# A hybrid decoder layer on one core: a head's loads issued a piece at a time, a branch's values in four groups, and the combination's first step pinned in program order

## The chip, the cores and the metric

The kernel runs on one core of a Trainium2 chip. The core has five engines that each work through a queue of instructions in order and wait for each other through semaphores: TensorE (PE, matrix products), VectorE (DVE), ScalarE (ACT), GpSimd (POOL) and SyncE (SP), whose queue issues nearly all DMA transfers. The metric is the device time of one execution in microseconds (us).

## The reference

One layer of a decoder with two kinds of token mixer, batch 1, 2048 tokens, width 1024, float32:

```python
nx = rmsnorm(h, attn_norm_g[l])
proj = jnp.einsum('bsd,dp->bsp', nx, w_in[l])
...
o_a = gla_mixer(...)                 # 4 heads, chunks of 64, low-rank forget gate
...
o_b = dilated_mixer(dq, dk_, dv_, rel_bias)   # 8 heads of 64
mixed = jnp.concatenate([o_a, o_b], axis=-1)
h = h + jnp.einsum('bsm,md->bsd', mixed, w_out[l])
nm = rmsnorm(h, mlp_norm_g[l])
a = jnp.square(jax.nn.relu(jnp.einsum('bsd,df->bsf', nm, w_ff1[l])))
h = h + jnp.einsum('bsf,fd->bsd', a, w_ff2[l])
return rmsnorm(h, final_norm_g)
```

The change lies in the dilated mixer. Each of its 8 heads has three branches (window, dilation) = (128, 1), (512, 4), (2048, 16): a query sees the keys at distances 0, d, 2d, ... up to the window. Each branch gives an output and the log-sum-exp of its logits, and the three are combined with weights from a softmax over those:

```python
for window, dilation in DSA_PATTERN:
    o, lse = dilated_branch(q, k, v, rel_bias, window, dilation)
    outs.append(o); lses.append(lse)
w = jax.nn.softmax(jnp.stack(lses, axis=0), axis=0)
return jnp.sum(w[..., None] * jnp.stack(outs, axis=0), axis=0)
```

## The kernel before, in words

The kernel has stages, one behind the other: the input projection, the attention (both mixers, interleaved; in the profiled execution from about 588 to 957 us), the output projection with the second norm, and the two products of the MLP. Matrix products that need float32 accuracy are split into a high and a low part and done as three matmuls (lines 67 to 69). The change touches the attention stage.

**Units.** A head's branch has 16 query windows of 128. The windows are grouped in `Unit`s: 4 windows for the branch of dilation 16 (called br 2), 2 for the others (br 1, br 0). A head has 20 units, the stage 160. The order is head by head, br 2, 1, 0; the last pair of heads has the order (6, br 2), (6, br 1), (7, br 2), (7, br 1) and then br 0 of both heads in turn.

**The loop** (L952 to L973) runs over k, a software pipeline of three steps: the scores of unit k + AHEAD (3), the transposition of the weights of unit k, and the products with the values of unit k − LAG (2). `Unit.scores` does two score matmuls for a window (L631 and L633: each of the split parts k1, k2 of the keys), and VectorE adds the bias and takes the minimum for the softmax (L643), ScalarE the exponential (L644). `Unit.transpose` transposes the weights on TensorE (L653) and copies them from PSUM by ScalarE (L660) or VectorE (L662). `Unit.values` multiplies with the values (L672), and VectorE copies four windows' result into `O` (L675). Between these stand the steps of the gated linear attention (GLA, lines 754 to 854).

**Calls by unit.** `at_unit(n, f)` (L903) has `f` called in the iteration that does the scores of unit n. `issue_later(n, ...)` (L737) has a transfer issued n iterations later. `first` is the first unit of a branch. So placed are:
- `load_head` (L524): six transfers of 512 KB on SyncE (the queries `qs` twice, two parts of the keys twice each), all at first − 13; the first branch of the next head needs them.
- `pack_q` (L574): four copies by GpSimd that order a head's queries for br 2 and br 1, at first − 4 to first − 1.
- `load_v` (L536): the values of a pair of heads for one branch, one transfer for br 2 and br 0, sixteen of 64 KB for br 1 (L547). Called for the next pair when a branch of the odd head ends (`after`, L892).
- `store_branch` (L681): the outputs of br 2 and br 1 of a pair go to DRAM (`boD`) 3 iterations after the branch's end, because the branches have different orders of tokens.
- `combine_load` (L691): two transfers of 528 KB read the two branches' outputs of half the tokens back, in order of tokens (`cmb`, L696).
- `combine` (L699): the weights. VectorE takes minima (L707, L708), subtracts (L710), ScalarE takes the exponential, VectorE sums and divides (L712 to L718); the small results lie in one tile, `small`. Then GpSimd multiplies (L724) and adds (L726), 128x512 elements at a time, and the result is stored for the output projection. The last group of the last pair runs on VectorE in place of GpSimd.

For pairs 0 to 2 the combination of a pair runs beside the next pair's first head, in two halves: loads at first − 2 and first + 5, six steps each from first + 3 and first + 10. For the last pair it runs beside br 0, in four groups of steps.

**What sets the order.** The instructions aren't run in the order in which the program records them: a scheduler reorders each engine's queue within the data dependences, by a model of its own. An instruction can thus stand ahead of those that were recorded before it. `tc.keep_in_program_order(x)` pins an instruction behind the one recorded before it on its engine. Large buffers come from a pool of 25 slots of equal size (`slot`), which all kinds of data share; a load into a slot waits until its last user has read it.

Of the kernel before, what the change touches and what calls it, by code (L numbers as in the profile page):

```python
# [10 lines left out]
F32 = mybir.dt.float32  # L11
FR = mybir.dt.float32r
I32 = mybir.dt.int32
AF = mybir.ActivationFunctionType
OP = mybir.AluOpType
AX = mybir.AxisListType

S = 2048
D = 1024
NT = S // 128  # L20
# [10 lines left out]
AHEAD, LAG = 3, 2  # L31
# [10 lines left out]
def emit(tc, a, stop=99):  # L42
    nc = tc.nc
    V, A, G, T, SP = nc.vector, nc.scalar, nc.gpsimd, nc.tensor, nc.sync
# [6 lines left out]
    def ps(tag):  # L51
        return psum.tile([128, 512], F32, name="ps_" + tag, tag=tag, bufs=BANKS[tag])

    def slot(name, dt=F32, n=SLOT):

        return up.tile([128, SLOT], dt, name=name, tag="u", bufs=25)[:, :n]

    def view(t, shape):
        n = int(np.prod(shape))
        names = "abcd"[:len(shape)]  # L60
        return t[:, :n].rearrange(f"p ({' '.join(names)}) -> p {' '.join(names)}", **dict(zip(names, shape)))
# [73 lines left out]
    qD = [dram.tile([2, 128, S], F32, name=f"qD{p}") for p in range(4)]  # L135
    kD = [dram.tile([2, 128, S], F32, name=f"kD{p}") for p in range(4)]
# [385 lines left out]


    def load_head(h):  # L524
        pr, hh = divmod(h, 2)
        qs, k1, k2 = slot("qs", FR, S), slot("k1", FR, S), slot("k2", FR, S)
        rows = slice(64 * hh, 64 * hh + 64)
        halves = [slice(64 * dup, 64 * dup + 64) for dup in range(2)]
        for dup, half in enumerate(halves):
            SP.dma_start(qs[half].bitcast(F32), qD[pr][dup, rows])  # L530
        for part, t in enumerate((k1, k2)):
            for half in halves:
                SP.dma_start(t[half].bitcast(F32), kD[pr][part, rows])
        return qs, k1, k2

    def load_v(pr, br):  # L536

        vt = view(slot("v"), (NT, 130))
        G.memset(vt[:, :, 0:130:129], 1.0)
        v = vt[:, :, 1:129]  # L540
        src = vD[:, pr * 128:pr * 128 + 128]
        if br == 0:
            SP.dma_start(v, src.rearrange("(t p) n -> p t n", p=128))
        elif br == 1:
            w = src.rearrange("(b x r i) n -> b x i r n", b=4, r=4, i=8)
            for n in range(NT):
                SP.dma_start(v[:, n], w[n // 4, :, :, n % 4])  # L547
        else:
            SP.dma_start(v, vN[:, pr * 128:pr * 128 + 128].rearrange("(p r) n -> p r n", r=16))
        return vt  # L550
# [130 lines left out]
    def store_branch(pr, br, O):  # L681
        dst = boD[pr][br - 1]
        if br == 1:
            issue_later(3, dst.rearrange("(b p r) n -> p b (r n)", b=4, r=4),
                        O.rearrange("p (b r) n -> p b (r n)", b=4))
        else:
            issue_later(3, dst.rearrange("(p r) n -> p (r n)", r=16), O.rearrange("p r n -> p (r n)"))
# [3 lines left out]
    def combine_load(pr, half):  # L691

        ts, u = slice(8 * half, 8 * half + 8), slot("cmb")
        R = [view(u[:, 1056 * b:], (8, 132)) for b in range(2)]
        for b in range(2):
            SP.dma_start(R[b], boD[pr][b].rearrange("(t p) n -> p t n", p=128)[:, ts])  # L696
        return R

    def combine(pr, t0, n, loaded, X):  # L699

        ts = slice(t0, t0 + n)
        R = [outs[pr, 0][:, ts], *[r[:, t0 % 8:t0 % 8 + n] for r in loaded]]
        at = small[:, t0 // 4 % 2 * 48:] if n == 4 else small
        E, Z, M = view(at, (3, n, 2)), view(at[:, 6 * n:], (2, n, 2)), view(at[:, 10 * n:], (n, 2))
        nm = [r[:, :, 130:132] for r in R]
        den = [r[:, :, 0:130:129] for r in R]
        V.tensor_tensor(M, nm[0], nm[1], op=OP.min)  # L707
        V.tensor_tensor(M, M, nm[2], op=OP.min)  # L708
        for b in range(3):
            V.tensor_tensor(E[:, b], M, nm[b], op=OP.subtract)  # L710
        A.activation(E, E, AF.Exp)
        V.tensor_tensor(Z[:, 0], E[:, 0], den[0], op=OP.mult)  # L712
        for b in (1, 2):
            V.tensor_tensor(Z[:, 1], E[:, b], den[b], op=OP.mult)
            V.tensor_tensor(Z[:, 0], Z[:, 0], Z[:, 1], op=OP.add)
        V.reciprocal(Z[:, 1], Z[:, 0])
        for b in range(3):
            V.tensor_tensor(E[:, b], E[:, b], Z[:, 1], op=OP.mult)  # L718
        yield
        for t in range(0, n, 4):  # L720
            rs = [r[:, t:t + 4, 1:129].rearrange("p t (h e) -> p t h e", h=2) for r in R]
            for b, r in enumerate(rs):
                wb = E[:, b, t:t + 4].unsqueeze(3).to_broadcast([128, 4, 2, 64])
                X.tensor_tensor(r, r, wb, op=OP.mult)  # L724
                if b:
                    X.tensor_tensor(rs[0], rs[0], r, op=OP.add)  # L726
                    yield
        if pr < 3 or t0 >= 8:
            issue_later(3 if pr < 3 else 2,
                        mixD[:, 512 + 128 * pr:640 + 128 * pr].rearrange("(t p) n -> p t n", p=128)[:, ts],  # L730
                        R[0][:, :, 1:129])

    due, clock = [], [0]

    def issue_later(n, *args):

        due.append((clock[0] + n, args))  # L737
# [128 lines left out]
            V.tensor_tensor(w[:, 1], raw, w[:, 0].bitcast(F32), op=OP.subtract)  # L866
            WO.append(w)

    pairs, outs = {0: load_head(0)}, {}
    for part in range(4):  # L870
        pack_q(0, 2, part)
    ring["pes"], ring["pts"] = view(slot("pe"), (4, 512)), view(slot("pt"), (4, 512))
    vs = {}
# [19 lines left out]
    def after(b):  # L893
        pr, hh = divmod(b.h, 2)
        if hh and b.br:
            store_branch(pr, b.br, b.O)
        if hh and pr < 3:
            vs[pr + 1, b.br] = load_v(pr + 1, b.br)

    units = []  # L900
    plan = {}
# [1 line left out]
    def at_unit(n, *f):  # L903
        plan.setdefault(n, []).append(f)
# [3 lines left out]
    def combine_at(pr, t0, n, at, steps):  # L908

        if at is not None:  # L910
            at_unit(at + AHEAD, lambda: got.update({(pr, t0 // 8): combine_load(pr, t0 // 8)}))

        def step():
            if (pr, t0) not in running:
                running[pr, t0] = combine(pr, t0, n, got[pr, t0 // 8], V if (pr, t0) == (3, 12) else G)
            next(running[pr, t0], None)

        for k in steps:
            at_unit(k + AHEAD, step)

    for pr in range(4):
        seq = [(hh, br) for hh in range(2) for br in (2, 1, 0)]
        if pr == 3:
            seq = [(0, 2), (0, 1), (1, 2), (1, 1), (0, 0), (1, 0)]
        for hh, br in seq:
            b = Branch()
            b.h, b.br = 2 * pr + hh, br
            m = 4 if br == 2 else 2
            first = len(units)
            if br:  # L930
                for part in range(4) if first else ():
                    at_unit(first - 4 + part, pack_q, b.h, br, part)
            if br == 2 and first:
                at_unit(first - 13, lambda h: pairs.update({h: load_head(h)}), b.h)
                if hh == 0:
                    for half in range(2):
                        combine_at(pr - 1, 8 * half, 8, first - 2 + 7 * half, [first + 3 + 7 * half + n for n in range(6)])
            if (pr, br) != (3, 0):
                for n in range(0, NT, m):
                    units.append(Unit(b, range(n, n + m)))  # L940
            elif hh:
                for n in range(0, NT, 4):
                    for w in (was, b):
                        units.extend(Unit(w, range(n + k, n + k + 2)) for k in (0, 2))
                for n, at in ((0, 8), (4, 11), (8, 14), (12, 18)):
                    combine_at(3, n, 4, first + 5 + n // 8 if n % 8 == 0 else None, [first + at + k for k in range(4)])
            was = b
    NU = len(units)
    for i in range(8):
# [179 lines left out]
    for at, t in enumerate(tiles):  # L1129
# [3 lines left out]
        h = u[:, 1]  # L1133
        p = [ps("a"), ps("a")]
# [159 lines left out]
    for at in range(7, len(jobs1)):  # L1294
# [12 lines left out]
        if at in (len(jobs1) - 4, len(jobs1) - 2):  # L1307
            n = (at + 4 - len(jobs1)) // 2
# [5 lines left out]
    for ph, (j, half) in enumerate(phases):  # L1314
        P = [bank() for _ in range(4)]
        for k in range(8):
            n = 8 * ph + k
            prep_a(n + 2)
            at = k + 8 * (1 - half)
# [51 lines left out]
def build(nc, inputs, stop=99):  # L1371
    arrays, aps = {}, {}
    for name in _INS:
        arrays[name] = np.ascontiguousarray(inputs[name])
    arrays.update(_constants())
    for name, v in arrays.items():
        aps[name] = nc.dram_tensor(name, v.shape, mybir.dt.from_np(v.dtype), kind="ExternalInput").ap()
    aps["out"] = nc.dram_tensor("out", (1, S, D), F32, kind="ExternalOutput").ap()
    with tile.TileContext(nc, schedule_with_timeline_sim=True) as tc:
        emit(tc, aps, stop)  # L1380
    return arrays
# [10 lines left out]
```

## Time and profile before

| | us |
|---|---|
| median of 3 runs | 2397.13 (2396.92 to 2399.54) |
| the profiled execution | 2398.99 |
| its span in the trace | 2397.2 |
| attention stage | 588.46 to 957.10 |

The span runs from the first to the last instruction that the profile shows; some 1.8 us of the execution lie outside. A line of the profile names the source line, the engine, the operation and the tiles (`out<-in`), then partitions x elements and type. In a timeline, the bracket at the end tells how long the engine was idle before the instruction, and what released it. In a list of waits the three numbers are us in total, times, and the longest. "SPq" is SyncE's queue, whose time on a DMA line is that of issuing, not of transfer.

### The profile page before, as it was taken

Reading aid. Unit: us, or ns where it says so; the run is one execution under the profiler, and the core shown is the slowest. Engines: PE = TensorE matmul, PEld = TensorE weight load, DVE = VectorE, ACT = ScalarE, POOL = GpSimd, SP = SyncE. Lnnn points to the kernel's source line nnn. Section 1 sums busy time; section 2 is a strip of 40 time slices with the busy share of each in tenths; the row PEclk is TensorE's granted clock in tenths of the full one; section 3 lists DMA queues with packets and bytes.
Section 4 is the critical chain, followed back from the end, with each engine's and each line's share of the span. In section 5 each row is a group of like instructions: output and inputs, shape, how many; then the busy total and the mean of one; then the engine's idle time right before and its main releaser. Section 6 shows DMA issues by size and latency. Waiting matters only on the chain.

```text
span 2397.2 us, 35124 instructions
## 1 busy us (share of the span) xinstructions
PE 2306.6 (96%) x12648; PEld 1989.9 (83%) x12648; DVE 1561.9 (65%) x2879; ACT 1148.0 (48%) x2181; POOL 583.3 (24%) x551
## 2 busy tenths in 40 slices
PE   6999998999999989999999999999999999999998
PEld 5877898779989988888788887888888888888886
DVE  6878666765667668445677778877773455556555
ACT  5565434533767657223455556555563333224323
POOL 5555435446566665100000000000000100001002
PEclk9999999999999999999999999999999999999999
DMA  6457664757888867468664447544467496457653
GB/s 159 120 164 230 213 189 136 206 166 194 213 193 226 225 174 241 154 201 267 203 206 145 145 149 242 176 162 157 155 203 274 155 315 208 168 170 248 217 167 106
DMA packets 342540, 458.13 MB, mean 191 GB/s; under 512 B 19620, under 2 KB 215733, under 8 KB 336094
## 3 DMA queue, kind: packets, MB, share of 16 engines
q1 hardware_dynamic: 313614, 413.15, 56.0%
q10 hardware_dynamic: 28752, 42.74, 5.2%
q8 instruction: 99, 1.62, 0.3%
q14 instruction: 75, 0.61, 0.1%
HBM read 293.51 MB, written 167.02 MB: 192 GB/s over the span
## 4 chain that ended last, share of the span: by engine, by line
PE 77%; DMA 8%; DVE 7%; issue 3%; ACT 3%; POOL 1%; SPq 1%; ACTq 0%; POOLq 0%; DVEq 0%
PE ps_a L67 8%; PE ps_a L68 8%; PE ps_a L69 8%; PE ps_c L67 7%; PE ps_c L69 7%; PE ps_c L68 7%; PE ps_d L67 4%; PE ps_d L69 4%; PE ps_d L68 4%; PE ps_a L672 4%; PE ps_o L67 3%; PE ps_o L68 3%; PE ps_o L69 3%; PE ps_d L653 2%; DMA cmb<-boD 2%
## 5 line engine op out<-in xcount | busy, mean ns | idle before, releaser
L1226 POOL TENSOR_TENSOR suma<-suma,gs 128x512 f32<-128x512 f32 x16 | 23.3, 1472 | 1152.6 <-ACT scr L1224 1152.5
L346 DVE TENSOR_TENSOR ca<-ra,ca 128x1024 fp32r<-128x1024 f32 x112 | 137.7, 1230 | 164.4 <-ACT ca L345 164.4
L345 ACT ACTIVATE ca<-ra 128x1024 fp32r<-128x1024 f32 x112 | 118.0, 1054 | 225.8 <-PE ps_c L69 185.4
L345 ACT ACTIVATE w1comb<-w1raw 128x512 fp32r<-128x512 f32 x224 | 139.6, 627 | 158.7 <-PE ps_c L69 57.7
L644 ACT ACTIVATE pe<-pe,O 128x256 f32<-128x256 f32 (+1 forms) x384 | 157.6, 454 | 89.1 <-DVE O L643 76.3
L672 PE MATMUL ps_a<-v,pt 128*128 128x65 f32 x1200 | 185.1, 258 | 13.3 <-DVE pt L662 8.5
L672 PEld LDWEIGHTS ps_a<-v,pt 128*128 128x128 f32 x1200 | 180.9, 200 | 16.1 <-DVE pt L662 9.5
L346 DVE TENSOR_TENSOR w1comb<-w1raw,w1comb 128x512 fp32r<-128x512 f32 x224 | 153.6, 689 | 53.4 <-ACT w1comb L345 53.2
L653 PE MATMUL ps_d<-ident,pe 128*128 128x128 f32 x600 | 160.9, 284 | 0.0
L643 DVE CUSTOM_DVE_ANT_0 pe<-ps_c,nb 128x256 f32<-128x256 f32 (+1 forms) x384 | 126.6, 360 | 43.4 <-PE ps_d L653 20.6
L204 DVE TENSOR_TENSOR wcomb<-wraw,wcomb 128x512 fp32r<-128x512 f32 (+2 forms) x84 | 101.2, 1210 | 70.3 <-ACT wcomb L202 68.8
L202 ACT ACTIVATE wcomb<-wraw 128x512 fp32r<-128x512 f32 (+2 forms) x126 | 96.3, 773 | 103.7 <-PE ps_a L69 20.8
L345 ACT ACTIVATE cb<-rb 128x1024 fp32r<-128x1024 f32 x56 | 59.4, 1061 | 158.0 <-PE ps_o L68 108.1
L67 PE MATMUL ps_c<-hb,w1comb 128*128 128x512 f32 x336 | 132.2, 393 | 2.8 <-ACT hb L345 2.8
L68 PE MATMUL ps_c<-hb,w1comb 128*128 128x512 f32 x336 | 132.2, 393 | 1.6 <-DVE w1comb L346 1.6
L69 PE MATMUL ps_c<-hb,w1comb 128*128 128x512 f32 x336 | 131.8, 392 | 0.0
L67 PE MATMUL ps_c<-cb,ca 128*128 128x512 f32 x336 | 130.8, 389 | 0.0
L68 PE MATMUL ps_c<-cb,ca 128*128 128x512 f32 x336 | 130.8, 389 | 0.0
L69 PE MATMUL ps_c<-cb,ca 128*128 128x512 f32 x336 | 130.8, 389 | 0.0
L653 PEld LDWEIGHTS ps_d<-ident,pe 128*128 128x128 f32 x600 | 111.1, 190 | 0.4
L94 POOL TENSOR_TENSOR stats<-stats,mhalf 128x1 f32<-128x1 f32 (+1 forms) x64 | 46.4, 730 | 259.3 <-DVE stats L93 216.1
L346 DVE TENSOR_TENSOR cb<-rb,cb 128x1024 fp32r<-128x1024 f32 x56 | 68.2, 1221 | 62.5 <-ACT cb L345 62.3
(351 smaller groups left out, 7330.2 us busy)
## 6 DMA issues: line engine op xcount, KB each, us to landing
ra<-actD SPq DMA_DIRECT2D x56, 1024.0 KB, 6.8
actD<-acc SPq DMA_DIRECT2D x192, 256.0 KB, 2.3
rb<-w_ff SPq DMA_DIRECT2D x72, 512.0 KB, 4.8
w1raw<-w_ff SPq DMA_DIRECT2D x32, 1024.0 KB, 7.3
k<-kD SPq DMA_DIRECT2D x32, 512.0 KB, 11.5
rb<-hTD SPq DMA_DIRECT2D x14, 1024.0 KB, 5.9
wraw<-w_in SPq DMA_DIRECT2D x48, 256.0 KB, 3.4
boD<-O SPq DMA_DIRECT2D x8, 1056.0 KB, 6.2
```

Source lines behind the costliest of these rows:

```text
L67: T.matmul(out, sh, mh, start=first, stop=False)
L68: T.matmul(out, sl, mh, start=False, stop=False)
L69: T.matmul(out, sh, ml, start=False, stop=last)
L94: G.tensor_tensor(r2, r, mhalf[:, :n], op=OP.pow)
L202: A.activation(hi, src, AF.Copy, scale=sc)
L204: V.tensor_tensor(lo, src, hi.bitcast(F32), op=OP.subtract)
L345: A.activation(hi, src, AF.Copy)
L346: V.tensor_tensor(lo, src, hi.bitcast(F32), op=OP.subtract)
L643: V.tensor_tensor_reduce(p, s, bias, scale=1.0, scalar=BIG, op0=OP.add, op1=OP.min, accum_out=nm)
L644: A.activation(p, p, AF.Exp, bias=nm, scale=-1.0)
L653: T.transpose(pb[:, i * 128:i * 128 + 128], src, ident)
L672: T.matmul(self.b.opsum[:, n % 4], self.pt[:, i * 128:i * 128 + 128], self.b.v[:, blk, cols], start=first, stop=last)
```

## The change

Six edits, all in the attention stage:

1. `load_head` becomes a generator that issues one of its six transfers a step. They are issued at first − 14, −13, −11, −9, −7 and −5, where all six stood at first − 13. Head 0's come all at once, as before.
2. The sixteen transfers of `load_v` for br 1 are issued in four groups of four, one unit apart, for pairs 1 to 3. For pair 0 they stay together.
3. The store of br 1's outputs is issued 2 iterations after the branch's end, not 3.
4. The first instruction of `combine` (L707) is pinned in program order.
5. For pairs 0 to 2, the combination's loads are issued at first − 3 and first + 3 (before: first − 2 and first + 5), and the second half's steps begin at first + 9 (before: first + 10). The first half's steps stay.
6. For the last pair, the loads are issued at first + 4 and first + 5 (before: first + 5 and first + 6), and the four groups' steps begin at 10, 13, 16, 18 units behind first (before: 8, 11, 14, 18).

```diff
     def load_head(h):
+
         pr, hh = divmod(h, 2)
-        qs, k1, k2 = slot("qs", FR, S), slot("k1", FR, S), slot("k2", FR, S)
         rows = slice(64 * hh, 64 * hh + 64)
-        halves = [slice(64 * dup, 64 * dup + 64) for dup in range(2)]
-        for dup, half in enumerate(halves):
-            SP.dma_start(qs[half].bitcast(F32), qD[pr][dup, rows])
-        for part, t in enumerate((k1, k2)):
-            for half in halves:
-                SP.dma_start(t[half].bitcast(F32), kD[pr][part, rows])
-        return qs, k1, k2
-
-    def load_v(pr, br):
+        t = pairs[h] = []
+        for name, of in (("qs", [qD[pr][0], qD[pr][1]]), ("k1", [kD[pr][0]] * 2), ("k2", [kD[pr][1]] * 2)):
+            t.append(slot(name, FR, S))
+            for dup in range(2):
+                SP.dma_start(t[-1][64 * dup:64 * dup + 64].bitcast(F32), of[dup][rows])
+                yield
+
+    def load_v(pr, br, later=lambda n, f, *args: f(*args)):
...
-            for n in range(NT):
-                SP.dma_start(v[:, n], w[n // 4, :, :, n % 4])
+            for b in range(4):
+                later(b, lambda b: [SP.dma_start(v[:, 4 * b + r], w[b, :, :, r]) for r in range(4)], b)
...
         if br == 1:
-            issue_later(3, dst.rearrange("(b p r) n -> p b (r n)", b=4, r=4),
+            issue_later(2, dst.rearrange("(b p r) n -> p b (r n)", b=4, r=4),
...
-        V.tensor_tensor(M, nm[0], nm[1], op=OP.min)
+        tc.keep_in_program_order(V.tensor_tensor(M, nm[0], nm[1], op=OP.min))
...
-    pairs, outs = {0: load_head(0)}, {}
+    pairs, outs = {}, {}
+    for _ in load_head(0):
+        pass
...
-            vs[pr + 1, b.br] = load_v(pr + 1, b.br)
+            vs[pr + 1, b.br] = load_v(pr + 1, b.br, lambda n, *f: at_unit(clock[0] + AHEAD + 1 + n, *f))
...
-                at_unit(first - 13, lambda h: pairs.update({h: load_head(h)}), b.h)
+                pieces = load_head(b.h)
+                for n in (14, 13, 11, 9, 7, 5):
+                    at_unit(first - n, lambda p: next(p), pieces)
                 if hh == 0:
                     for half in range(2):
-                        combine_at(pr - 1, 8 * half, 8, first - 2 + 7 * half, [first + 3 + 7 * half + n for n in range(6)])
+                        combine_at(pr - 1, 8 * half, 8, first - 3 + 6 * half, [first + 3 + 6 * half + n for n in range(6)])
...
-                for n, at in ((0, 8), (4, 11), (8, 14), (12, 18)):
-                    combine_at(3, n, 4, first + 5 + n // 8 if n % 8 == 0 else None, [first + at + k for k in range(4)])
+                for n, at in ((0, 10), (4, 13), (8, 16), (12, 18)):
+                    combine_at(3, n, 4, first + 4 + n // 8 if n % 8 == 0 else None, [first + at + k for k in range(4)])
```

In the changed kernel the lines from 536 to 868 of the kernel before bear numbers lower by one (L707 becomes L706), those behind them numbers higher by one to three.

## The prediction

> **What bounds the kernel now.** I read the page's first part and the chain first, to see which engine carries the end.
>
> ```profile
> PE 2306.6 (96%) x12648; PEld 1989.9 (83%) x12648; DVE 1561.9 (65%) x2879; ACT 1148.0 (48%) x2181; POOL 583.3 (24%) x551
> ...
> PE 77%; DMA 8%; DVE 7%; issue 3%; ACT 3%; POOL 1%; SPq 1%; ACTq 0%; POOLq 0%; DVEq 0%
> ```
>
> TensorE is busy 96% of the span, so only its idle time, and time at a lower clock, can be won without removing matmuls; the change removes none. It touches the attention stage alone. So next I read TensorE's busy time in that stage, in three undisturbed stretches of it, and in the four stretches where it stood (columns: us, PE busy, instructions, granted clock, DMA share, GB/s).
>
> ```profile
> 588.46:957.10 368.64, 347.56 (x3006) 0.95 0.81 214
> 600.00:680.00 80.00, 80.00 (x724) 1.00 0.83 205
> 700.00:780.00 80.00, 80.00 (x720) 1.00 0.80 206
> 800.00:860.00 60.00, 60.00 (x533) 1.00 0.93 232
> 686.00:696.00 10.00, 4.27 (x26) 0.66 1.17 289
> 782.00:796.00 14.00, 10.85 (x62) 0.63 0.67 193
> 860.00:874.00 14.00, 6.22 (x34) 0.63 1.13 308
> 946.00:954.00 8.00, 5.76 (x29) 0.65 0.55 216
> ```
>
> Of the stage's 368.64 us TensorE is idle 21.1, nearly all in the last four rows; elsewhere it has no gap. The rows' clock (0.63 to 0.66) says that it also ran slowly behind each gap. The list of waits of TensorE in that stage, then that of VectorE, name what it stood for.
>
> ```profile
> PE ps_a L672 <- DVE pt L662: 8.5, 4, 5.7
> PE ps_c L631 <- DVE small L710: 7.8, 1, 7.8
> PE ps_a L672 <- ACT pt L660: 2.6, 3, 2.2
> PE ps_a L672 <- DVE O L675: 2.2, 1, 2.2
> PE ps_c L631 <- POOL qp L585: 1.0, 1, 1.0
> ```
>
> ```profile
> DVE small L707 <- DMA cmb<-boD: 25.7, 6, 11.2
> DVE O L675 <- PE ps_a L672: 25.0, 32, 2.7
> ```
>
> TensorE waits for VectorE, and VectorE for the re-read branch results (`cmb<-boD`): its first instruction of the combination, L707, stands at the head of a queue that also holds the score copies (L643) and transposed weights (L662) TensorE needs. The timeline of VectorE gives the three large waits, the chain of waits the loads behind them.
>
> ```profile
> 690.48 0.62 DVE L707 TENSOR_TENSOR small<-O,cmb 128x16 f32<-128x16 f32 x1 [7.07 <-DMA cmb<-boD]
> ...
> 782.79 0.64 DVE L707 TENSOR_TENSOR small<-O,cmb 128x16 f32<-128x16 f32 x1 [4.49 <-DMA cmb<-boD]
> ...
> 867.74 0.17 DVE L707 TENSOR_TENSOR small<-O,cmb 128x16 f32<-128x16 f32 x1 [11.20 <-DMA cmb<-boD]
> ```
>
> ```profile
> 674.27 16.19 DMA cmb<-boD
> ...
> 767.62 16.81 DMA cmb<-boD
> ...
> 861.76 5.96 DMA cmb<-boD
> ```
>
> **The change part by part.** *What the three gaps cost.* Undisturbed, TensorE issues 724 instructions in 80 us, 0.111 us each. By that, the 26, 62 and 34 of the three gap rows need 2.9, 6.9 and 3.8 us of their 10, 14 and 14: lost are 7.1 + 7.1 + 10.2 = **24.4 us**. (Mixes differ and instructions across an edge count, so I put ±3 on it.) The idle time alone is 5.7 + 3.2 + 7.8 = 16.7 (rows' us less busy); the rest is low clock.
>
> Here a rule of the Trainium skill can be weighed against the rows: "TensorE: Matmul & The Clock Gate", section "Part 1: The HAM clock gate", gives half rate after at least one idle window of about 3.4 us, and full rate again after as long a busy one. By that, the middle gap, whose idle time is 3.2 us in all, would keep its clock and cost 3.2 us only, and the sum would be about 20; this trace shows 0.63 over that gap, so I go by the rows.
>
> *Gaps 1 and 2: loads moved ahead.* SyncE's timeline shows why they were late.
>
> ```profile
> 670.43 1.12 SPq L530 DMA_DIRECT2D qs<-qD  x2
> 671.60 2.62 SPq L533 DMA_DIRECT2D k<-kD  x4
> 674.27 6.71 SPq L696 DMA_DIRECT2D cmb<-boD  x2
> ```
>
> ```profile
> k<-kD SPq DMA_DIRECT2D x28, 512.0 KB, 11.9
> cmb<-boD SPq DMA_DIRECT2D x16, 528.0 KB, 6.4
> qs<-qD SPq DMA_DIRECT2D x14, 512.0 KB, 8.8
> woraw<-w_out SPq DMA_DIRECT2D x8, 512.0 KB, 5.7
> ```
>
> The six loads of a head, 3 MB, stand directly ahead of the second half's two, 1 MB; landing takes 16.2 us against a median of 6.4. After the change the half is loaded two units earlier (first+3, was first+5), and a head's loads come in pieces from unit −14 on. In the built programs the two `cmb` loads stand in front of the head's loads for the second half of pairs 0 and 1, where they stood behind. A unit is 2.2 us (the stage's 368.64 over 160 units, less the gaps). The load of gap 1 is then issued at about 674.3 − 3.8 (the six issues ahead) − 4.4 = 666 and, at the median, there at 672.5, against VectorE's need from 683.4: 11 us to spare, and at 16.2 us still 1. In gap 2 the same working gives about 14, and the pin adds to it: L707 stands behind the 230th score window instead of the 224th, some 5 us later. Both gaps go: −14.2.
>
> *Gap 3: the branch store moved ahead of the value loads.*
>
> ```profile
> 838.84 14.32 SPq L547 DMA_DIRECT2D v<-vD  x14
> ...
> 855.38 1.17 SPq L743 DMA_DIRECT2D boD<-O  x1
> ...
> 861.76 0.36 SPq L696 DMA_DIRECT2D cmb<-boD  x1
> ```
>
> The sixteen 64 KB value loads of the next pair take 14.3 us of SyncE's queue just ahead of the store of branch 1, which the combination reads back. With four at a time, one unit apart, and the store at two units instead of three, the store passes most of them: issued about 842 instead of 855.4. Store 6.2 us, load 6.0 to 6.4: there at about 854.5, against a need at 856.5 by the old place of L707, and later by the pin (308 windows instead of 302, 5 us). Some 7 us to spare: −10.2. Moving the value loads costs nothing that I see; they are needed a whole pair later.
>
> *The pin.* It adds no work; VectorE asks later, never earlier. Behind L707 everything of the combination moves: in the built order from 100, 204, 302 score windows to 116, 228, 308, the second halves from 126, 224, 308 to 128, 230, 320. The two halves thus stand closer together, and their weights share one small tile: the second half's subtraction (L710) must wait until GpSimd has multiplied with the first's. That is a **new wait** of VectorE, with the score copies queued behind it and TensorE behind those.
>
> ```profile
> L585 POOL CAST qp<-qs 128x512 fp32r<-128x512 f32 x58 | 58.8, 1083 | 8.3 <-DMA qs<-qD 4.7 <-PE ps_a L672 3.7
> L726 POOL TENSOR_TENSOR O<-O,cmb 128x512 f32<-128x512 f32 x27 | 36.4, 1361 | 0.1
> L724 POOL TENSOR_TENSOR cmb<-cmb,small 128x512 f32<-128x512 f32 x29 | 29.5, 1044 | 0.0
> ```
>
> A half has six multiplications, 6.3 us; the built order puts the three subtractions 1, 5 and 7 windows (0.9 us each) behind the last weight at pair 1, where 2.1, 4.2 and 6.3 us would be asked: up to 1.2 us of wait, up to 5.5 with a `pack_q` of four (4.3 us) ahead. A VectorE wait costs TensorE less than its length: 7.07, 4.49 and 11.20 above became 5.7, 3.2 and 7.8, so 1.3 to 3.4 us are swallowed. Bounds for three boundaries: 0 and 3 × (5.5 − 1.3) × 24.4/16.7 = 18; I take +3, near the lower, since the 1.2 us would be swallowed whole.
>
> *A head in pieces.* The last K piece is issued 5 units, 11 us, ahead of its first score instead of 13. A 512 KB load lands in 5.7 us by the least crowded row, in 11.9 where six stand together. Now at most two do: 0, with 1 × 7 heads as upper end.
>
> *The end of the stage.* The fourth row lost 8 − 29 × 0.111 = 4.8 us behind this wait of VectorE and this slowed instruction.
>
> ```profile
> 932.69 0.36 DVE L707 TENSOR_TENSOR small<-O,cmb 128x8 f32<-128x8 f32 x2 [1.99 <-DMA cmb<-boD]
> ...
> 945.10 1.24 DVE L715 TENSOR_TENSOR small<-small 128x8 f32<-128x8 f32 x1
> ```
>
> The last pair's steps now start two units later and its loads one earlier, so the 1.99 goes. But VectorE's first steps fall behind 379 windows instead of 373, and three of four groups behind the last: GpSimd's chain for the first tiles (1.0 + 1.0 + 1.0 + 1.4 + 1.4 a group) is later, and the out-projection, which needs them, can stand up to 4 us. Between −4.8 and +4: I take −1.5.
>
> Sum: −14.2 − 10.2 + 3 − 1.5 = **−23**. The profiled execution took 2399.0 us (span 2397.2 and 1.8 around it), so 2376; it lies 1.9 above the median of the runs, 2397.1, which makes the forecast **2374**.
>
> **The rivals.**
>
> *One gap stays, or the new waits are dear.* The spare time of gap 1 is 1 us if its load still takes 16 us, and that of gap 3 rests on a store and a load in series. For: the DMA share is over 1 in two of the gap rows. Against: those rows hold the 3 MB that now come later. One gap left gives 2381 to 2384, the GpSimd wait at its upper end 2389.
>
> *Bytes are the bound.* The same bytes are moved, so a load put ahead pushes another back, and a gap reappears behind a K or GLA load: 2397. For: the gap rows move 289 and 308 GB/s. Against: the stage moves 214 on average, so there is room on both sides of each gap. The Trainium skill's "DMA: Bandwidth & Descriptors", section "Specifications", puts a core's HBM limit at about 358 GB/s, near those rows, and no issue order lifts that; by it alone the change would give nothing in the crowded microseconds, and the stage's 214 says they need not be crowded.
>
> *Slower: the last K piece comes late at every head.* Its lead falls from 28 to 11 us, and at the start of each of seven heads TensorE would wait directly for it. At the 16.5 us that the crowded `cmb` loads took, it waits 5.5 us, with the slow clock (24.4/16.7) 8, seven times 56: about 2430. It eats the whole gain from (23/7)/1.46 = 2.3 us of lateness on, a landing of 13.3 us. Against: nothing but its twin and the value groups stands near it.
>
> *It doesn't do what it says.* A scheduler may still put another instruction at the head of VectorE's queue. The built order shows only moves to later, so I add this to the case of no gain.
>
> **How the numbers follow.** All three gaps go, new waits 0 to 8 us: 2368 to 2381, chance 0.62. One gap or dear new waits, 2381 to 2392: 0.21. The end gains as well, below 2368: 0.04. No gain, 2392 to 2402: 0.07. Slower, by the late K piece: 0.06. Predicted is 2374; the range 2368 to 2391 leaves out 0.04 + 0.07 + 0.06 and the edge of the second case. A measurement of this kernel tells about 0.2% (4.8 us) from no change: faster 0.87, same 0.07, slower 0.06.
>
> **What would show it.** Right: L707 no longer waits for `cmb<-boD` over 1 us before the last pair; TensorE's waits for L662 and L710 are gone; the clock is 1.00 from 600 to about 920; the stage is 20 to 26 us shorter, and the stages before and after it are unchanged. Wrong: VectorE's subtraction (now L709) waiting for GpSimd, with a TensorE gap right behind; TensorE waiting for `k<-kD` at a head's first scores; a larger gap at the end, in which the last transposes wait for GpSimd's sum.

## The result, and the profile after

| | median of the runs (us) | profiled execution | span |
|---|---|---|---|
| before | 2396.92 (2391.55 to 2399.54, 5 runs) | 2398.99 | 2397.2 |
| after | 2410.85 (2407.51 to 2414.81, 5 runs) | 2412.10 | 2410.3 |

The change made the kernel **slower**: the ratio is 1.0058, with a 95% interval of 1.0044 to 1.0072. The forecast was 2374, and its range (2368 to 2391) misses the result by 20 us. The profiled execution of before lies some 2 us above that kernel's median, so I take what an edit costs from medians (between runs of different comparisons by way of their ratios to the kernel before), and use traces only for where the time sits.

What was forecast for VectorE's waits behind the three gaps did happen. The first rows of VectorE's list of waits in the changed kernel's attention stage (us in total, times, longest) no longer hold the re-read results, which stood first with 25.7 us:

```profile
DVE O L674 <- PE ps_a L671: 35.5, 31, 3.1
DVE pe L642 <- PE ps_d L652: 20.8, 24, 6.1
```

Something else took their place. TensorE's list of waits from 588 to 990 us, in the changed kernel:

```profile
PE ps_c L632 <- DMA k<-kD: 10.5, 3, 6.9
PE ps_a L68 <- DVE mT L346: 7.3, 1, 7.3
PE ps_a L671 <- ACT pt L659: 3.3, 4, 2.0
PE ps_a L67 <- DVE O L674: 3.2, 1, 3.2
PE ps_a L671 <- DVE pt L661: 3.2, 2, 2.6
PE ps_a L67 <- ACT mT L345: 1.7, 1, 1.7
```

Two things are new: a wait for **keys**, inside the stage, and a wait for **`mT`**, the split input of the output projection, at the stage's end. The last value matmuls of the attention show how much each weighs. They start at 959.9 us before and 957.6 after; from there to the end of the span it takes 1437.3 us before and 1452.7 after. So the stage won only 2.3 us although VectorE's waits behind its three gaps are gone, and what follows lost 15.4.

*The keys.* TensorE's timeline in the changed kernel shows the three places, each at the first scores of a head:

```profile
618.18 0.38 PE L632 MATMUL ps_c<-k,qp 128*128 128x256 f32 x1 [1.49 <-DMA k<-kD]
...
797.46 0.36 PE L632 MATMUL ps_c<-k,qp 128*128 128x256 f32 x1 [2.12 <-DMA k<-kD]
...
876.83 0.55 PE L632 MATMUL ps_c<-k,qp 128*128 128x256 f32 x1 [6.93 <-DMA k<-kD]
```

The chain of waits has the transfers that ended them (start, duration):

```profile
605.06 12.98 DMA k<-kD
...
784.71 12.61 DMA k<-kD
...
868.95 7.74 DMA k<-kD
```

Two took 12.6 and 13.0 us to land. The last took 7.7, but was issued only 7.9 us before TensorE went on. SyncE's timeline shows what stood ahead of it, and of the second one:

```profile
771.79 8.97 SPq L776 DMA_DIRECT2D gla<-glD  x1
...
783.62 1.95 SPq L532 DMA_DIRECT2D k<-kD  x2
...
861.79 7.12 SPq L777 DMA_DIRECT2D gla<-gqD  x1
...
868.95 0.77 SPq L532 DMA_DIRECT2D k<-kD  x1
```

These are loads of the gated attention, whose buffers were not free yet. SyncE's queue runs in order, so it stood for 9.0 and 7.1 us, and the key pieces stood behind. SyncE's list of waits names whom it waited for: the second of these for GpSimd's `pack_q` copies. Its first row is longer: a head's own loads waited for TensorE to free their buffers, though at none of the three places.

```profile
SPq L532 <- PE ps_c L632: 21.7, 4, 14.3
...
SPq L776 <- PE ps_d L652: 11.1, 5, 9.0
...
SPq L777 <- POOL qp L584: 7.1, 1, 7.1
```

*The end.* VectorE's timeline behind the last value matmuls: the fourth group's first step, its subtractions, its products and sums (they run on VectorE), and only then the split of the second half of the first token tile (`mT<-ps_d`), for which TensorE waits:

```profile
962.45 0.80 DVE L706 TENSOR_TENSOR small<-O,cmb 128x8 f32<-128x8 f32 x1
...
965.78 1.94 DVE L709 TENSOR_TENSOR small<-small,cmb 128x8 f32<-128x8 f32 x2
...
973.12 0.69 DVE L723 TENSOR_TENSOR O<-O,small 128x512 f32<-128x512 f32 x1
...
974.92 1.42 DVE L725 TENSOR_TENSOR O<-O,cmb 128x512 f32<-128x512 f32 x2
976.25 0.68 DVE L346 TENSOR_TENSOR mT<-ps_d,mT 128x512 fp32r<-128x512 f32 x1
```

```profile
976.99 0.79 PE L68 MATMUL ps_a<-wo,mT 128*128 128x512 f32 x1 [7.26 <-DVE mT L346]
```

Four waits of TensorE stand behind the last value matmuls: 3.2 us for `O`, 0.9 for GpSimd's sum, then 1.7 and 7.3 for `mT`. Together they are 13.1 of the 15.4 us; the kernel before has no wait there up to 1000 us.

### The profile page after: what moved, and what is told of

It reads as the page before. It is cut to its first block, busy times and chain, and to the rows that moved or that the text cites. A ratio compares the mean times of both kernels' runs of the same rounds, so it can differ in the third digit from the quotient of the medians.

```text
span 2410.3 us, 35124 instructions
## 1 busy us (share of the span) xinstructions
PE 2310.8 (96%) x12648; PEld 1991.5 (83%) x12648; DVE 1569.1 (65%) x2879; ACT 1147.3 (48%) x2181; POOL 584.9 (24%) x551
## 4 chain that ended last, share of the span: by engine, by line
PE 75%; DMA 9%; DVE 8%; issue 3%; ACT 3%; POOL 2%; SPq 1%; ACTq 0%; POOLq 0%; DVEq 0%
PE ps_a L68 8%; PE ps_a L67 8%; PE ps_a L69 8%; PE ps_c L67 7%; PE ps_c L69 7%; PE ps_c L68 7%; PE ps_d L67 4%; PE ps_d L68 4%; PE ps_d L69 4%; PE ps_o L67 3%; PE ps_o L68 3%; PE ps_o L69 3%; PE ps_a L671 2%; DMA k<-kD 2%; PE ps_d L652 2%
## 5 line engine op out<-in xcount | busy, mean ns | idle before, releaser
L67 PE MATMUL ps_a<-wo,mT 128*128 128x512 f32 x256 | 102.6, 401 | 5.6 <-DVE O L674 3.2
## 6 DMA issues: line engine op xcount, KB each, us to landing
k<-kD SPq DMA_DIRECT2D x32, 512.0 KB, 10.5
```

Source lines behind the costliest of these rows:

```text
L67: T.matmul(out, sh, mh, start=first, stop=False)
```

## The experiments

Each was compared with the kernel before on the same chip; the medians of before there were 2393.88 (first four), 2395.96 (next four) and 2396.42 (last four). The changed kernel was measured apart from them (before there: 2396.92), so it is compared with these runs by the ratios to before, in us of some 2396. "Score windows" tell where the combination's first step stands in VectorE's queue of the built kernel: behind how many of the 384 score copies. Six numbers are the two halves of pairs 0 to 2, four the groups of the last pair.

**The last pair unpinned**

```diff
-        tc.keep_in_program_order(V.tensor_tensor(M, nm[0], nm[1], op=OP.min))
+        first_op = V.tensor_tensor(M, nm[0], nm[1], op=OP.min)
+        if pr < 3:
+            tc.keep_in_program_order(first_op)
```

> The changed kernel with the pin on the combination's first step taken away for the last pair only (pairs 0 to 2 keep it). Theory A, the pin and the later steps together push the last pair's combination behind the last scores, and the output projection waits for it: the time falls by the some 22 us that the end lost (the first 376 windows were about 9 us ahead of before, the end 13 behind), to about 2388, and the waits of TensorE on the copy of the mixed output behind 960 us go; three waits for keys, 10.5 us, stay. Rival B, the end is late because the loads and the gated attention's last chunks are late, whatever the pin: 2405 to 2411, the waits stay.

Measured: 2397.43 (ratio 1.0010, 0.9998 to 1.0021), by the ratios some 11 us below the changed kernel. The four groups stand at 374, 374, 378 and 384 instead of 379, 384, 384 and 384. Without the pin the order of every engine is the same whether the steps begin at 8, 11, 14 or at 10, 13, 16: the scheduler lifts them anyway, so edit 6 acts only through the pin. The wait for `mT` is gone, but the waits for keys are larger (17.5 us in two places). VectorE's timeline has the split ahead of the fourth group's products (this kernel's lines are two higher):

```profile
962.52 0.68 DVE L346 TENSOR_TENSOR mT<-ps_d,mT 128x512 fp32r<-128x512 f32 x1
...
968.72 0.69 DVE L725 TENSOR_TENSOR O<-O,small 128x512 f32<-128x512 f32 x1
```

Theory A holds, but the time is 9 us above what it expected; 7 us more stand in the waits for keys (17.5 instead of 10.5).

**The last pair's steps as before, pinned**

```diff
-                for n, at in ((0, 10), (4, 13), (8, 16), (12, 18)):
+                for n, at in ((0, 8), (4, 11), (8, 14), (12, 18)):
```

> The changed kernel with the last pair's steps where they were before (8, 11, 14, 18 instead of 10, 13, 16, 18), the pin kept. Theory A: the first two groups come four windows earlier in VectorE's queue (375 and 380 instead of 379 and 384), the other two stay behind the last scores, so a part of the end's loss goes: 2396 to 2404. If the shift of the steps were the whole cause and the pin none: about 2388. Rival B: 2405 to 2411.

Measured: 2408.51 (1.0059, 1.0041 to 1.0076), no different from the changed kernel. The first two groups stand four windows earlier (375, 380), and nothing came of it: TensorE still waits 7.5 us for `mT`. So these four windows don't count, and my expectation of a part of the gain missed.

**A head's loads all at once**

```diff
-                for n in (14, 13, 11, 9, 7, 5):
+                for n in (13,) * 6:
```

> The changed kernel with all six loads of a head issued at first - 13 again; the other edits stay. Theory K, the last K piece is issued too late: TensorE's three waits for keys (10.5 us and some 4 of half clock) go, the time falls to about 2397. Rival L, the head's six loads in one block again delay the combination's loads: VectorE waits for those again, 5 to 20 us of the gaps come back, 2400 to 2420.

Measured: 2387.49 (0.9969, 0.9959 to 0.9979), by the ratios some 21 us below the changed kernel: theory K holds, with more than its 14 us. No wait for keys is left, and VectorE waits 0.2 us for the re-read results: rival L falls.

The last value matmuls start at 935.5 us, 24.4 before those of the kernel before. That this is the very sum of the three gaps is chance, since the order differs too: 16 matmuls of the gated attention, which stood ahead of the last values, stand behind them here. A better mark is the 661st of the stage's 768 score matmuls, which lies behind all three gaps: it starts at 874.9 us here and at 890.0 before, so by then some 15 us are won. Against the rest of the 24.4 stand other waits. The longest, at 849 us, where the kernel before has none, is for the gated attention's step on ScalarE (the granted clock from 845 to 855 us is 0.67); it is the first row of TensorE's list:

```profile
PE ps_o L834 <- ACT gla L826: 3.9, 1, 3.9
```

Behind the last values it takes 1449.1 us to the end, against 1437.3, a part of it for the matmuls that moved there.

**Both undone**

> The changed kernel with both undone: the last pair as before (steps, loads, no pin) and a head's six loads at first - 13. Theories A and K together: 2411 - 22 - 14, about 2375. If the pieces are what freed the combination's loads (rival L), the gaps come back: 2385 to 2397.

The edits are those of the first and the third experiment, and the last pair's steps and loads as before. Measured: **2384.12** (0.9959, 0.9944 to 0.9974), the fastest of all: by the ratios 10 us faster than before, some 24 faster than the change. TensorE's list of waits from 580 to 1000 us begins:

```profile
PE ps_a L671 <- DVE pt L661: 6.3, 7, 2.2
PE ps_o L836 <- ACT gla L828: 3.6, 1, 3.6
PE ps_d L652 <- DVE pt L661: 2.4, 1, 2.4
```

It is above the expected 2375: of the 36 us that I had taken off the changed kernel, some 24 came. Against this kernel, on the same chip, the pieces cost 13.3 us (first experiment) and the last pair's edits 3.4 (third), the latter within what these intervals can tell. Both together cost some 24, by the ratios of the changed kernel as by the second experiment on this chip. So the two make each other worse by some 7 to 9 us, an estimate that the intervals leave open by some 6 us to either side.

**One edit alone, three times.** The pin for pairs 0 to 2, added to the kernel before:

> The kernel before with one thing added: the combination's first step pinned for pairs 0 to 2 (edit 4, without the last pair). Loads stay as late as they were. Theory P, VectorE asked too early: the pin puts the first step 16, 24 and 6 score windows later in the first halves and 5, 20 and 16 in the second halves (0.9 us each), so the middle gap goes, the first and the third are halved: about 2381 to 2385. Theory E, only earlier loads can close the gaps: 2394 to 2398, and VectorE's waits for the re-read results stay at 20 us or more.

Measured: 2396.65 (1.0004, 0.9994 to 1.0015). The first step stands at 116, 131, 228, 244, 308, 324, and VectorE still waits, since the loads are as late as they were:

```profile
DVE small L707 <- DMA cmb<-boD: 16.6, 3, 9.1
DVE small L710 <- DMA cmb<-boD: 4.2, 3, 2.8
```

The earlier loads alone:

```diff
-  first - 2 + 7 * half, [first + 3 + 7 * half + n for n in range(6)]
+  first - 3 + 6 * half, [first + 3 + 6 * half + n for n in range(6)]
```

> The kernel before with edit 5 alone: the combination's loads one and two units earlier, no pin. Theory P: the scheduler lifts the first step as far as the loads (10 score windows earlier in the second halves of pairs 0 and 1), so the waits stay: 2388 to 2398. Theory E: the gaps of pairs 0 and 1 close, the third stays: about 2380.

Measured: 2398.52 (1.0006, 0.9995 to 1.0018). The scheduler lifts the first step to 100, 116, 198, 214, 300, 308: ten windows earlier in the second halves of pairs 0 and 1, where the loads are two units earlier. The waits are back:

```profile
DVE small L707 <- DMA cmb<-boD: 14.4, 7, 5.1
DVE small L708 <- DMA cmb<-boD: 6.6, 3, 4.8
```

The values in four groups and the earlier store (edits 2 and 3) alone:

> The kernel before with edits 2 and 3 alone: the sixteen value loads in four groups, the store of branch 1 at two units. If the store's place in SyncE's queue was the cause of the third gap, that gap (10 us) goes and the two others stay: about 2384 to 2387. If the scheduler lifts the first step of the combination accordingly (it stands 6 windows earlier here), half of it stays: about 2390.

Measured: 2397.07 (1.0008, 0.9999 to 1.0017). The third gap did not go: L707 stands at 296 instead of 302 there, and waits longer, 13.7 us:

```profile
864.16 0.18 DVE L707 TENSOR_TENSOR small<-O,cmb 128x16 f32<-128x16 f32 x1 [13.68 <-DMA cmb<-boD]
```

None of the three can be told from no change.

**The pieces earlier**

```diff
-                for n in (14, 13, 11, 9, 7, 5):
+                for n in (16, 15, 14, 12, 10, 8):
```

> The changed kernel with the last pair as before and a head's loads still in six pieces, but three units earlier at their end: at first - 16, -15, -14, -12, -10, -8. Theory K, only the lateness of the last piece costs: no waits of TensorE for keys, the time is that of the kernel with all six at once, about 2384. Rival Q, pieces as such cost, because each stands behind other transfers and waits in SyncE's queue: 10 us or more of waits for keys stay, 2392 to 2400.

Measured: 2388.82 (0.9974, 0.9964 to 0.9984), 8.6 us below the kernel with the late pieces (first experiment, whose built order at the last pair is that of this kernel). So the lateness of the last pieces costs most of it. The rest, some 4 us above the kernel with all six at once, lies within the two intervals, and the trace, of the slowest of this kernel's runs, can't place it. There is no wait for keys; TensorE's list begins:

```profile
PE ps_o L836 <- ACT gla L828: 6.7, 2, 4.0
PE ps_a L671 <- DVE pt L661: 4.4, 4, 2.2
```

**Two of the three edits.** Pin and earlier loads:

> The kernel before with edits 4 (pairs 0 to 2) and 5 together: the pin and the earlier loads; values, store and a head's loads as before. If each gap needs both, VectorE asking later and the load coming earlier, the first two gaps go and the third, behind the store, is halved: about 2385 to 2388. If more than the two is needed: 2394 to 2398.

Measured: 2393.43 (0.9986, 0.9977 to 0.9995). Of VectorE's waits for the re-read results 9.2 us are left, 6.2 of them in one place: the third gap, behind the store. Loads, values and store, no pin:

> The kernel before with edits 2, 3 and 5 together and no pin: all transfers of the combination earlier, the first step free to be lifted. If the scheduler's lifting eats what the loads win (it stands at 100, 116, 196, 214, 300, 308 score windows here, against 116, 128, 222, 224, 308, 320 with the pin), the waits for the re-read results stay: 2392 to 2398. If the pin isn't needed once the loads are early: about 2384.

Measured: 2394.05 (0.9988, 0.9979 to 0.9998). Here the waits are all left:

```profile
DVE small L707 <- DMA cmb<-boD: 23.4, 6, 9.6
DVE small L708 <- DMA cmb<-boD: 6.4, 2, 4.7
```

Both gain some 3 us, all of the edits 2 to 5 together (fourth experiment, the pin for pairs 0 to 2) 10.

**Which pinned groups make the end late.** The pin off groups 1 and 2 of the last pair only (`pr < 3 or t0 >= 8`):

> The changed kernel with the pin taken off the first two of the last pair's four groups only. Theory M, the end is late because the pinned first groups push the split of the first tile's second half for the output projection behind all four groups in VectorE's queue: here that split stands ahead of the third and the fourth group, so the time falls to about 2397, as without any pin on the last pair. Rival N, the late third and fourth groups (384 windows, as in the changed kernel) cost by themselves: 2405 to 2411.

Measured: 2396.05 (0.9996, 0.9984 to 1.0008). The pin off groups 3 and 4 only (`pr < 3 or t0 < 8`):

> The changed kernel with the pin taken off the third and fourth of the last pair's groups only. Theory M: the first groups stay pinned at 379 windows and the first tile's split still stands behind all four groups: 2405 to 2411, the wait of TensorE for that split of 7 us stays. Rival N: about 2397.

Measured: 2410.13 (1.0048, 1.0032 to 1.0064), with the wait of the changed kernel in its list:

```profile
PE ps_a L68 <- DVE mT L346: 7.6, 1, 7.6
```

Theory M holds on both sides: 14 us hang on the pin of the first two groups, none on that of the others. In the trace of the first of the two, the split `mT<-ps_d` stands behind the third group's subtractions, ahead of its sums and of the fourth group; in the second, in the changed kernel and in the second experiment it stands behind all four. The place alone isn't the cost: with the pin on pairs 0 to 2 and the earlier loads ("Two of the three edits") it stands behind the fourth group too, and TensorE waits 2.2 us. There the split starts 10 us behind the start of the last value matmuls, in the changed kernel 19. So the pin costs by both together, the place of the split and the lateness of the groups ahead of it.

## Why the prediction was wrong

**The step that failed: "A head in pieces ... 0, with 1 × 7 heads as upper end".** It measured some 21 us (third experiment against the changed kernel) or 13 (first against fourth). I compared a lead of 11 us with the landing times of two rows, took 5.7 and not 11.9, and said that at most two pieces would stand together. In the changed kernel the key loads land in 10.8 us at the median:

```profile
k<-kD SPq DMA_DIRECT2D x28, 512.0 KB, 10.8
```

A head's pieces had left their own block, but other transfers stand around them. And the lead is counted from the unit at which the program issues, not from the moment at which SyncE does. I had written that nothing but its twin and the value groups stands near the last piece; the gated attention's loads, which wait for GpSimd or TensorE to free their buffers, held the queue for 9.0 and 7.1 us. That it is the lateness that costs, and hardly the pieces as such, the run with earlier pieces shows. My slower rival had the right mechanism, with too small a chance (0.06), and asked for it at all seven heads; three were enough, with the second failure beside them.

**The second: the end, "between −4.8 and +4: I take −1.5".** With the pieces it measured +11 (changed kernel against the first experiment) to +14 (the last two experiments against each other); without them +3.4, which the intervals can't tell from nothing. I had looked at how late GpSimd's chain and the transposes would be, which was the smaller part: TensorE waits 0.9 us for GpSimd's sum. What I left out is what stands behind the combination in VectorE's queue, the splits of the output projection's input. The first tile's second split fell behind all four groups, and the small operations of those groups take long there: 0.16 us each by themselves, 0.90 to 0.97 beside GpSimd's products. VectorE's timeline, then GpSimd's, in the changed kernel:

```profile
949.35 0.16 DVE L714 TENSOR_TENSOR small<-small 128x8 f32<-128x8 f32 x1
...
951.40 0.90 DVE L714 TENSOR_TENSOR small<-small 128x8 f32<-128x8 f32 x1
952.34 0.97 DVE L713 TENSOR_TENSOR small<-small,cmb 128x8 f32<-128x8 f32 x1
```

```profile
952.24 2.04 POOL L723 TENSOR_TENSOR cmb<-cmb,small 128x512 f32<-128x512 f32 x2
```

The Trainium skill, "SBUF — State Buffer", section "SBUF: two separate sides", says that VectorE (with two SBUF inputs) and GpSimd take a shared port for a whole instruction each, and the other one waits. The trace agrees: each small operation takes about as long as one of GpSimd's products beside it (1.02).

**The three gaps, −24.4: VectorE's waits went, but some 15 us were won, and not as a sum of separate edits.** With the pieces undone, TensorE is 15 us ahead behind the third gap (third experiment); the sum had no term for waits that the earlier stage would meet, such as the 3.9 us for ScalarE. And I gave gaps 1 and 2 to the earlier loads and gap 3 to the store, while alone neither wins anything. The scheduler puts L707 as early as its model lets it, so an earlier load is followed by an earlier asking, and a pin alone asks later but finds the load still late. Of the sets that were run, only the pin, the loads, the value groups and the store together close all three. The pin with the store but without the earlier loads wasn't run, nor the store apart from the value groups.

**The new wait of VectorE for GpSimd, +3**: nearly nothing. The list of waits has it with 0.3 us.

```profile
DVE small L709 <- POOL O L723: 0.3, 1, 0.3
```

**The clock.** The prediction preferred the row of the middle gap to the rule of the Trainium skill ("TensorE: Matmul & The Clock Gate", section "Part 1: The HAM clock gate"). The changed kernel bears that out. Its windows on TensorE around the three waits for keys (us, busy, clock, DMA share, GB/s) alone would fit the rule:

```profile
615.00:620.00 5.00, 3.51 (x34) 1.00 1.02 213
...
795.00:800.00 5.00, 2.88 (x24) 1.00 1.11 236
...
870.00:875.00 5.00, 0.00 (x0) 0.71 1.13 246
875.00:880.00 5.00, 3.17 (x17) 0.50 1.05 283
```

Waits of 1.5 and 2.1 us left the clock at 1.00, the one of 6.9 us halved it. But a single wait of 2.6 us in the same trace lowered it as well:

```profile
701.84 0.69 PE L671 MATMUL ps_a<-v,pt 128*128 128x65 f32 x2 [2.63 <-DVE pt L661]
```

```profile
700.00:705.00 5.00, 3.16 (x17) 0.64 0.02 8
705.00:710.00 5.00, 5.00 (x36) 0.68 0.16 48
```

So did the single wait of 2.2 us in the prediction's fourth row (0.65), and the two of 2.2 and 1.0 us of its middle gap (0.63). In the fourth experiment a wait of 2.2 us at 691 us left the clock at 1.00. So in these traces a wait of 2 to 3 us can lower the clock or not, and the rule by an idle window of 3.4 us doesn't tell which; what decides, these runs don't show.

Open stays why pieces and pinned end together cost some 7 to 9 us more than each by itself. In the kernel with all six loads at once, the built order has the first tile's second split ahead of the fourth group's products in spite of the pin; that would explain it, but no run varied it by itself. Also not tried was a run in which the gated attention's loads are moved away from in front of the key pieces, so how much of the lateness is the queue and how much the landing is read from the trace alone.

## What to carry to other kernels

Before a load is moved closer to its use, take the lead from the queue that issues it: what stands ahead of it there may wait for an engine, and here one held instruction (7 to 9 us) cost as much as the spread of landing times. Where a scheduler places instructions, an earlier load and a pinned user are one edit, not two; measured apart, both look worthless. And a pin near the end of a stage also pins what the next stage needs from the same engine, so look at the first instruction of the next stage in that queue, not only at the work that is pinned.

## What the runs showed of the hardware that was not expected

A 512 KB load of keys took from 4.9 to 13.8 us to land in one and the same execution of the changed kernel, and 15.4 in one case in which SyncE was held for 7.6 us while it issued it. The median is 10.8, so a lead of 11 us was no more than the median, without a margin. The combination's loads landed no later for being asked for earlier: in 5.9 us at the median, against 6.4 before. And single waits of TensorE of 2 to 3 us were followed by a lower clock in some places (0.64 behind 2.6 us) and not in others (1.00 around 2.1 and 2.2 us).
